# Moving part of a column sum from TensorE to VectorE in a prefix-sum kernel that streams 285 MB

## The chip, the cores and the metric

One core of a Trainium2 chip runs the kernel. The metric is device time in microseconds from start to end of one execution; the profile's span is some 1.7 us shorter, as it runs from the first to the last instruction. Ratios are computed as the mean time of one kernel's fast runs over the mean of the other's fast runs of the same rounds on the same chip, so they are not quite the ratios of the medians quoted beside them.

## The reference

```python
def reference(x):                      # x: (4, 4224, 4224) float32
    ps = np.cumsum(np.cumsum(x, axis=1), axis=2)
    diag = np.diagonal(ps, axis1=1, axis2=2)
    return np.cumsum(diag, axis=1).astype(np.float32)     # (4, 4224)
```

Every element of x with row and column up to i counts in the i-th diagonal value. All of x has to be read: 4 x 4224 x 4224 x 4 bytes = 285.5 MB.

## The kernel before

Columns are in 11 groups of 384. A batch is loaded as five strips of 768 rows, six rows to a partition, and a half strip of 384 rows, converted to bfloat16 on the way, into three strip buffers. The last batch is cut differently at its end, to shorten the work after the last byte.

```python
NBUF = 3
strips = ctx.enter_context(tc.tile_pool(name="strips", bufs=NBUF))
...
def load_rows(o, b, r0):                          # issued on GpSimd's queue
    f = o.shape[1]
    nc.gpsimd.dma_start(
        out=o, in_=x[b, r0 : r0 + f * P, :].rearrange("(p f) w -> p f w", f=f)
    )
...
def add_up(strip, f, r0, acc, um, wp=0, ws=None):
    nw = f * P // GW
    g = r0 // GW
    hi = r0 + f * P
    for j in range(g + nw, NG):                   # TensorE: column sums right of the block
        for q in range(f):
            columns(j, 0, GW, strip[:, q, j * GW : (j + 1) * GW], q > 0)
    ...
    mu = mup.tile([P, f, f * P], BF16, name=f"mu{f}")
    block = strip[:, :, r0:hi]                    # VectorE: the block on the diagonal
    nc.vector.tensor_mul(out=mu, in0=block, in1=um)
    nc.vector.tensor_sub(out=block, in0=block, in1=mu)
    for h in range(nw):
        for q in range(f):
            columns(g + h, 0, GW, mu[:, q, h * GW : (h + 1) * GW], q > 0)
    for q in range(f):                            # ScalarE: row sums of the left part
        if ws > wp:
            act_sum(acc[:, q, 0:1], strip[:, q, wp:ws])
    row_sums(acc[:, :, 1], strip[:, :, ws:hi])    # VectorE: row sums of the rest
...
# end of the last batch
weigh_b(dtot, weights, start=True)
weigh_a(ones_col[0:1], c12[0:1, 1, :], start=True)
weigh_b(ones_col[0:1], c12[0:1, 1, M0:])
...
nc.vector.tensor_copy(out=yl[:, :M0], in_=fin_a)
nc.sync.dma_start(out=out[b, T0 : T0 + M0].unsqueeze(0), in_=yl[:, :M0])
```

`columns` is a matmul with a one-hot selector, which adds the column sums of 384 columns to one row of `d` in PSUM. Six rows per partition take six of them. VectorE's `row_sums` is the last reader of most strips; when it is done, the buffer is free and GpSimd issues the load of the strip three places on.

Of the kernel before, what the change touches and what calls it, by code (L numbers as in the profile page):

```python
# [8 lines left out]
FP32 = mybir.dt.float32  # L9
# [8 lines left out]
def kernel(  # L18
# [14 lines left out]
    nc = tc.nc  # L33
# [3 lines left out]
    P = 128  # L37
    F = 3
    F2 = 2 * F
    GW = P * F  # L40
    NG = N // GW
# [7 lines left out]
    consts = ctx.enter_context(tc.tile_pool(name="consts", bufs=1))  # L49
    strips = ctx.enter_context(tc.tile_pool(name="strips", bufs=NBUF))  # L50
    mup = ctx.enter_context(tc.tile_pool(name="mup", bufs=1))
# [19 lines left out]
    def strip_tile():  # L71
        return strips.tile([P, F2, N], BF16, name="strip")

    def load_rows(o, b, r0):
# [4 lines that stand above are left out]
# [8 lines left out]
    sel = consts.tile([P, 2 * NG - 1], BF16, name="sel")  # L87
# [3 lines left out]
    def upper_mask(f):  # L91

        um = consts.tile([P, f, f * P], BF16, name=f"um{f}")
        nc.vector.memset(um, 1.0)  # L94
        nc.gpsimd.affine_select(  # L95
            out=um,
            in_=um,
            compare_op=ALU.is_gt,
            fill=0.0,
            base=0,  # L100
            pattern=[[-1, f], [1, f * P]],
            channel_multiplier=-f,
        )
        return um

    um6 = upper_mask(F2)
    um3 = upper_mask(F)
# [3 lines left out]
        out=um1,  # L111
        in_=um1,
# [10 lines left out]
        out=ident,  # L123
        in_=ident,
# [13 lines left out]
    def counted(name, rows, width, pieces):  # L138

        ti = consts.tile([P, GW], I32, name="counted")[:rows, :width]  # L140
        for c0, c1, base, step, cm in pieces:
            nc.gpsimd.iota(
                ti[:, c0:c1],
                pattern=[[step, c1 - c0]],
                base=base,
                channel_multiplier=cm,
            )
        tf = consts.tile([rows, width], FP32, name=name)
        nc.gpsimd.tensor_copy(out=tf, in_=ti)
        return tf  # L150
# [6 lines left out]
    def between_groups(name, turned):  # L157
# [25 lines left out]
    weights = counted("weights", P, GW, [(0, GW, 1, 1, -1)])  # L183
    nc.gpsimd.affine_select(
        out=weights,
        in_=weights,
# [12 lines left out]
        out=steps, in_=steps, scalar=2, op=ALU.arith_shift_right  # L199
# [7 lines left out]
    def matmul(o, lhsT, rhs, start=False):  # L207
        nc.tensor.matmul(  # L208
            o, lhsT=lhsT, rhs=rhs, start=start, stop=False, skip_group_check=True
        )  # L210

    def matmul_on(o, lhsT, rhs):

        te = nc.tensor
        te.add_instruction(  # L215
            mybir.InstMatmult(
                start_tensor_calc=False,
                stop_tensor_calc=False,
                tile_position=(0, 0),
                tile_size=(P, P if lhsT.shape[-1] > 64 else 32),  # L220
                bass_skip_group_check=True,
                ldweights=False,
                name=nc.get_next_instruction_name(),
                engine=te.engine,
                ins=[
                    te.lower_ap(rhs, opt=False),
                    te.lower_ap(lhsT, opt=False, for_matmul_weights=True),
                ],
                outs=[te.lower_ap(o)],
            )  # L230
        )
# [3 lines left out]
    ones_col = consts.tile([P, 1], FP32, name="ones_col")  # L235
# [11 lines left out]
    def act_sum(acc, src):  # L247
        w = src.shape[-1]
        dump = dumpool.tile([P, 2176], BF16, name="dump")
        nc.scalar.activation(  # L250
            out=dump[:, :w], in_=src, func=ACT.Copy, accum_out=acc
        )

    def row_sums(acc, src):
        nc.vector.reduce_sum(out=acc, in_=src, axis=AX.X)  # L255
# [18 lines left out]
    def masked(o, i, m, acc):  # L274
        nc.vector.scalar_tensor_tensor(  # L275
            out=o,
            in0=i,
            scalar=1.0,
            in1=m,
            op0=ALU.mult,  # L280
            op1=ALU.mult,
            accum_out=acc,
        )

    def scalar_cols(r0):

        return r0 * 9 // 16 // 32 * 32
# [22 lines left out]
    for b in range(B):  # L310
        whole = b < LB
        t0 = 0 if whole else 1
        r6, r3 = rows6[b % 2], rows3[b % 2]
        d = psum_d.tile([NG, GW], FP32, name="d")
# [6 lines left out]
        def row_of(j):  # L321
            return (j + t0) % NG

        def columns(j, lo, hi, rhs, same=False):


            k = row_of(j)
            lhsT = sel[:, NG - 1 - k : 2 * NG - 1 - k]
            if same:
                matmul_on(d[:, lo:hi], lhsT, rhs)  # L330
                return
            matmul(d[:, lo:hi], lhsT, rhs, start=first[0])
            first[0] = False

        def add_up(strip, f, r0, acc, um, wp=0, ws=None):


            nw = f * P // GW
            g = r0 // GW
            hi = r0 + f * P  # L340
            for j in range(g + nw, NG):
                for q in range(f):
                    columns(j, 0, GW, strip[:, q, j * GW : (j + 1) * GW], q > 0)
            if ws is None:
                ws = scalar_cols(r0)
            mu = mup.tile([P, f, f * P], BF16, name=f"mu{f}")
            block = strip[:, :, r0:hi]
            nc.vector.tensor_mul(out=mu, in0=block, in1=um)  # L348
            nc.vector.tensor_sub(out=block, in0=block, in1=mu)  # L349
            for h in range(nw):  # L350
                for q in range(f):
                    columns(g + h, 0, GW, mu[:, q, h * GW : (h + 1) * GW], q > 0)
            for q in range(f):
                if ws > wp:
                    act_sum(acc[:, q, 0:1], strip[:, q, wp:ws])
            row_sums(acc[:, :, 1], strip[:, :, ws:hi])

        acc6 = smalls.tile([P, NS, F2, 2], FP32, name="acc6")
# [10 lines left out]
        for s in range(ns):  # L369
            strip = prefetched.pop(0) if prefetched else None  # L370
            if strip is None:
                strip = strip_tile()
                load_rows(strip, b, s * F2 * P)
            add_up(strip, F2, s * F2 * P, acc6[:, s], um6)
            if not whole and s == 0:
                diag_b = last.tile([P, P], BF16, name="diag_b")
                nc.gpsimd.dma_start(out=diag_b, in_=x[b, TB:N, TB:N])
            if not whole and s == 1:
                row_sums(hs[:, 2:3], diag_b)
                masked(hmu[:, 2, :P], diag_b, um1[:, :P], hu[:, 2:3])  # L380
                nc.vector.tensor_sub(out=dtot, in0=hs[:, 2:3], in1=hu[:, 2:3])
                for h in range(3):
                    columns(LG, h * P, GW, hmu[:, h, : GW - h * P], h > 0)
        a6 = acc6[:, :ns]
        sum_up(a6)
        for h in range(2):
            ps = slice(h * HP, (h + 1) * HP)
            k = row_of(h)
            nc.vector.tensor_copy(  # L389
                out=r6[ps, k : k + 2 * ns : 2, :], in_=a6[ps, :, :, 1]  # L390
            )

        strip = strip_tile()
# [5 lines left out]
        else:  # L399
# [8 lines left out]
            wp, ws = 1280, 1280 + 1536  # L408
# [6 lines left out]
        if not whole:  # L415

            strip = strip_tile()
# [7 lines left out]
            for sb, c0, c1 in (  # L425
# [6 lines left out]
                r0 = TB + sb * R  # L432
                nc.gpsimd.dma_start(
                    out=part_b[:, sb, c0:c1],
                    in_=x[b, r0 : r0 + R, :TB].rearrange("r (k c) -> r k c", k=4)[
                        :, :, c0:c1
                    ],
# [18 lines left out]
        c12 = smalls.tile([NG, 2, GW], FP32, name="c12")  # L456
# [9 lines left out]
        for i, src in enumerate((d, c12[:, 0, :])):  # L466
            nc.vector.tensor_tensor_scan(  # L467
                out=c12[:, i, :],
# [8 lines left out]
            out=out[b, : j1 * GW].rearrange("(g i) -> g i", i=GW),  # L477
            in_=c12[t0:NG, 1, :],
# [5 lines left out]
        M0 = 2 * P  # L484
        E0 = GW - R
        fin_a = psum_s.tile([1, M0], FP32, name="fin_a")
        fin_b = psum_s.tile([1, P], FP32, name="fin_b")
        fin_e = psum_s.tile([1, R], FP32, name="fin_e")
        yl = last.tile([1, GW], FP32, name="yl")
        ye = last.tile([1, R], FP32, name="ye")  # L490

        def weigh_a(rows, w, start=False):

            matmul(fin_a, rows, w[..., :M0], start=start)

        def weigh_b(rows, w, r0=0, start=False):

            matmul(fin_b[:, r0:], rows, w[..., : P - r0], start=start)
# [7 lines left out]
        by = last.tile([P, P], FP32, name="by")  # L506
        nc.scalar.copy(out=by, in_=by_ps)
        weigh_b(dtot, weights, start=True)
        weigh_a(ones_col[0:1], c12[0:1, 1, :], start=True)
        weigh_b(ones_col[0:1], c12[0:1, 1, M0:])  # L510


# [1 line left out]
        arows = last.tile([P, 2], FP32, name="arows")  # L514
        nc.vector.tensor_add(out=arows, in0=asum[:, :, 0], in1=asum[:, :, 1])
        weigh_b(ones_col, by)
        weigh_a(arows[:, 0:1], weights)
        matmul(fin_a[:, P:], arows[:, 1:2], weights[:, :P])
        weigh_b(arows[:, 0:1], weights[:, M0:])
        weigh_b(arows[:, 1:2], weights[:, P:])  # L520
# [5 lines left out]
        pair_sum(bsum[:, 0, 1:2], part_b[:, 1, 512:])  # L526
        for i in (1, 0):
            weigh_b(bsum[:, 0, i : i + 1], weights4, R)
        nc.vector.tensor_copy(out=yl[:, :M0], in_=fin_a)
        nc.sync.dma_start(  # L530
            out=out[b, T0 : T0 + M0].unsqueeze(0), in_=yl[:, :M0]
        )
# [2 lines left out]
        for i in (1, 0):  # L535
# [8 lines left out]
            out=out[b, T0 + M0 : T0 + E0].unsqueeze(0), in_=yl[:, M0:E0]  # L544
# [35 lines left out]
```

## Time and profile before

| | before |
|---|---|
| median of the first three runs | 667.75 us (667.42 to 669.84) |
| span of the profiled run | 666.1 us |
| busy: VectorE / TensorE / ScalarE / GpSimd | 333.8 / 209.2 / 136.1 / 31.3 us |
| read from HBM | 285.47 MB |

The DMA row is the only one that is full. The page's first part (busy time, share of the span, instructions of each engine) and its summary of the chain that ended last name VectorE most often:

```profile
PE 209.2 (31%) x998; PEld 99.5 (15%) x998; DVE 333.8 (50%) x163; ACT 136.1 (20%) x219; POOL 31.3 (5%) x59
...
DVE 44%; another core or an unknown queue 41%; DMA 13%; PE 2%; issue 1%; DVEq 0%; POOLq 0%
```

Half of VectorE's time is idle, and the 41% "unknown" are waits for strips.

### The profile page before, as it was taken

To read this page: it belongs to the slowest core of one execution; us is meant where nothing else is said; L and a number is where in the kernel's file an instruction comes from. 1 tells how busy PE (TensorE), PEld (TensorE's weight loads), DVE (VectorE), ACT (ScalarE), POOL (GpSimd) and SP (SyncE) were. 2 spreads that over 40 slices of the span, in tenths; PEclk is the share of its full clock that TensorE was granted. 3 is DMA by queue.
4 is the path that set the end of the run, shared out by engine and by line. 5 is a ranking of instruction groups with operands and counts; after the bars stand their busy time and mean duration, and the time that the engine had idled before them with its cause. 6 is when DMAs were issued, how large, how long until landed. Compare 5 with 4: busy or idle time off the path is not lost.

```text
span 666.1 us, 2585 instructions
## 1 busy us (share of the span) xinstructions
PE 209.2 (31%) x998; PEld 99.5 (15%) x998; DVE 333.8 (50%) x163; ACT 136.1 (20%) x219; POOL 31.3 (5%) x59
## 2 busy tenths in 40 slices
PE   0071522403118153140320724414022253250428
PEld 0030211201003021010110312201011021120203
DVE  3160625456916153454782524436388343352766
ACT  0001121406300103040630020304063002030434
POOL 7000000000000000000000000000000000001000
PEclk9995857566558585765655958567565595765759
DMA  9999999999999999999999999999999999999998
GB/s 203 219 219 219 213 216 213 213 218 219 219 220 218 219 216 213 219 213 216 218 219 217 219 218 216 217 216 219 213 218 218 218 219 217 216 217 216 218 207 163
DMA packets 7673, 143.25 MB, mean 215 GB/s; under 512 B 704, under 2 KB 1004, under 8 KB 2156
## 3 DMA queue, kind: packets, MB, share of 16 engines
q0 software_dynamic: 7296, 142.47, 99.9%
q1 hardware_dynamic: 364, 0.61, 0.3%
q8 instruction: 8, 0.13, 0.1%
q14 instruction: 5, 0.04, 0.0%
HBM read 285.47 MB, written 0.07 MB: 429 GB/s over the span
## 4 chain that ended last, share of the span: by engine, by line
DVE 44%; another core or an unknown queue 41%; DMA 13%; PE 2%; issue 1%; DVEq 0%; POOLq 0%
DVE acc L255 27%; DMA strip<-in_x_dram 13%; DVE mu L348 7%; DVE strip L349 7%; DVE c L467 1%; PE d L208 1%; PE fold_a L215 0%; DVE pu L255 0%; DVE c L275 0%; PE fold_a L208 0%; PE fin_b L208 0%; PE fin_a L208 0%; DVE acc L364 0%; DVE rows L389 0%
## 5 line engine op out<-in xcount | busy, mean ns | idle before, releaser
L250 ACT ACTIVATE dump<-strip 128x416 bf16<-128x416 bf16 (+6 forms) x108 | 124.4, 1151 | 520.8 <-DMA strip<-in_x_dram 518.1
L348 DVE TENSOR_TENSOR mu<-strip,um 128x4608 bf16<-128x4608 bf16 (+1 forms) x24 | 52.4, 2183 | 307.5 <-DMA strip<-in_x_dram 307.4
L255 DVE TENSOR_REDUCE acc<-strip 128x6 f32<-128x4608 bf16 (+6 forms) x23 | 196.0, 8523 | 0.8
L208 PE MATMUL d<-strip,sel 128*11 128x384 bf16 x102 | 42.3, 415 | 375.8 <-DMA strip<-in_x_dram 375.8
L215 PEld LDWEIGHTS <-sel 128*11 128x11 bf16 x703 | 72.2, 103 | 502.8 <-issue 469.8
L215 PE MATMUL d<-strip,sel 128*11 128x384 bf16 x501 | 131.9, 407 | 0.0
L349 DVE TENSOR_TENSOR strip<-strip,mu 128x4608 bf16<-128x4608 bf16 (+1 forms) x24 | 52.4, 2183 | 1.0
L215 PE MATMUL d<-mu,sel 128*11 128x384 bf16 x200 | 43.9, 352 | 0.0
L76 POOL DMA_DIRECT2D strip<-in_x_dram x24 | 16.5, 688 | 543.4 <-DVE acc L255 281.4
L208 PE MATMUL d<-mu,sel 128*11 128x384 bf16 x43 | 15.6, 363 | 45.7 <-DVE mu L348 45.7
L250 ACT ACTIVATION_READ_ACCUMULATOR dump<-strip 128x1 f32 x108 | 20.1, 186 | 0.0
L208 PEld LDWEIGHTS <-sel 128*11 128x11 bf16 x146 | 14.6, 100 | 18.9 <-issue 10.1
L208 PE MATMUL d<-ident,rows 128*11 128x128 f32 x24 | 5.2, 380 | 16.8 <-DVE rows L398 16.8
L94 DVE MEMSET um<- 128x4608 bf16 (+1 forms) x2 | 4.9, 2458 | 1.1 <-issue 1.1
L208 PEld LDWEIGHTS d<-ident,rows 128*11 128x11 f32 x24 | 2.6, 119 | 18.9 <-DVE rows L398 11.7
L95 POOL TENSOR_SCALAR_AFFINE_SELECT um<-um 128x4608 bf16<-128x4608 bf16 (+1 forms) x2 | 5.2, 2613 | 2.4 <-DVE um L94 2.4
L208 PE MATMUL d<-halves,rows 128*11 128x64 f32 x48 | 5.3, 288 | 0.0
L255 DVE TENSOR_REDUCE pu<-d 11x1 f32<-11x384 f32 x4 | 2.2, 546 | 5.7 <-PE d L208 5.7
L208 PEld LDWEIGHTS d<-halves,rows 128*11 128x11 f32 x48 | 4.8, 128 | 1.3 <-issue 1.1
L215 PEld LDWEIGHTS <-ident_h 128*128 128x128 bf16 x18 | 2.1, 114 | 13.7 <-issue 12.7
L467 DVE TENSOR_TENSOR_SCAN c<-ones_row,carry,c 11x384 f32<-11x384 f32 x4 | 4.0, 1005 | 0.1
L467 DVE TENSOR_TENSOR_SCAN c<-ones_row,carry,d 11x384 f32<-11x384 f32 x4 | 4.0, 1001 | 0.1
(100 smaller groups left out, 51.3 us busy)
## 6 DMA issues: line engine op xcount, KB each, us to landing
strip<-in_x_dram POOLq DMA_DIRECT2D x19, 6336.0 KB, 76.5
strip<-in_x_dram POOLq DMA_DIRECT2D x5, 3168.0 KB, 59.7
strip<-in_x_dram POOLq DMA_DIRECT2D x1, 1080.0 KB, 49.9
strip<-in_x_dram POOLq DMA_DIRECT2D x1, 768.0 KB, 52.9
strip<-in_x_dram POOLq DMA_DIRECT2D x3, 256.0 KB, 54.1
head<-in_x_dram SPq DMA_DIRECT2D x1, 528.0 KB, 3.7
strip<-in_x_dram POOLq DMA_DIRECT2D x1, 192.0 KB, 43.2
strip<-in_x_dram POOLq DMA_DIRECT2D x1, 64.0 KB, 28.6
```

The source lines that it names most:

```text
L76: nc.gpsimd.dma_start(out=o, in_=x[b, r0 : r0 + f * P, :].rearrange("(p f) w -> p f w", f=f))
L94: nc.vector.memset(um, 1.0)
L95: nc.gpsimd.affine_select(out=um, in_=um, compare_op=ALU.is_gt, fill=0.0, base=0, pattern=[[-1, f], [1, f * P]], channel_multiplier=-f,)
L208: nc.tensor.matmul(o, lhsT=lhsT, rhs=rhs, start=start, stop=False, skip_group_check=True)
L215: te.add_instruction(mybir.InstMatmult(start_tensor_calc=False, stop_tensor_calc=False, tile_position=(0, 0), tile_size=(P, P if lhsT.shap ...
L250: nc.scalar.activation(out=dump[:, :w], in_=src, func=ACT.Copy, accum_out=acc)
L255: nc.vector.reduce_sum(out=acc, in_=src, axis=AX.X)
L348: nc.vector.tensor_mul(out=mu, in0=block, in1=um)
L349: nc.vector.tensor_sub(out=block, in0=block, in1=mu)
L467: nc.vector.tensor_tensor_scan(out=c12[:, i, :], data0=ones_row, data1=src, initial=carry[:, i : i + 1], op0=ALU.mult, op1=ALU.add,)
```

## The change

The intent is to take work from TensorE. In strips two to five of the three whole batches (12 strips), the first column group to the right of the diagonal block is summed over its six rows by VectorE, and one float32 matmul replaces six bfloat16 ones. At the end, a small matmul that added the scanned row is replaced by an addition in the copy that VectorE makes anyway.

```diff
+    sel_f = consts.tile([P, 2 * NG - 1], FP32, name="sel_f")
+    nc.vector.tensor_copy(out=sel_f, in_=sel)
...
-            for j in range(g + nw, NG):
+            for j in range(g + nw + by_rows, NG):
...
+            if by_rows:
+                rowed = mup.tile([P, GW], FP32, name="rowed")
+                row_sums(
+                    rowed,
+                    strip[:, :, hi : hi + GW].rearrange("p q c -> p c q"),
+                )
             for h in range(nw):
                 for q in range(f):
                     columns(g + h, 0, GW, mu[:, q, h * GW : (h + 1) * GW], q > 0)
+            if by_rows:
+                k = row_of(g + nw)
+                matmul(d, sel_f[:, NG - 1 - k : 2 * NG - 1 - k], rowed)
...
-            add_up(strip, F2, s * F2 * P, acc6[:, s], um6)
+            add_up(
+                strip, F2, s * F2 * P, acc6[:, s], um6, by_rows=whole and s > 0
+            )
...
-        weigh_a(ones_col[0:1], c12[0:1, 1, :], start=True)
...
-        weigh_a(arows[:, 0:1], weights)
+        weigh_a(arows[:, 0:1], weights, start=True)
...
-        nc.vector.tensor_copy(out=yl[:, :M0], in_=fin_a)
+        nc.vector.tensor_add(out=yl[:, :M0], in0=fin_a, in1=c12[0:1, 1, :M0])
```

More of the change, by code (lines that the diff above doesn't have):

```diff
@@ L333, in columns, with add_up @@
             first[0] = False
-        def add_up(strip, f, r0, acc, um, wp=0, ws=None):
+        def add_up(strip, f, r0, acc, um, wp=0, ws=None, by_rows=False):
             nw = f * P // GW
```

## The prediction

> **What bounds the kernel now.** I began with the page's slices, because the shares of busy time (VectorE 50%, TensorE 31%) name no engine that is full.
>
> ```profile
> DVE  3160625456916153454782524436388343352766
> DMA  9999999999999999999999999999999999999998
> GB/s 203 219 219 219 213 216 213 213 218 219 219 220 218 219 216 213 219 213 216 218 219 217 219 218 216 217 216 219 213 218 218 218 219 217 216 217 216 218 207 163
> ```
>
> The DMA engines are at nine tenths or more in all but the last slice, and the rate hardly moves. VectorE swings from 0 to 9 tenths under it without a mark: the eleventh slice, with VectorE at 9, has 219 GB/s, the fourth, with VectorE at 0, has 219 too. Those GB/s count bfloat16 bytes as written; what is read is float32, twice as much. x is 4 x 4224 x 4224 x 4 bytes = 285.5 MB, which the page confirms as 285.47 MB of HBM reads. Over the 666.1 us span that is 429 GB/s.
>
> Next the table of stretches, cut where strips arrive (start:end, length, busy time and count of PE, PEld, DVE, ACT, POOL, then clock, DMA share, GB/s):
>
> ```profile
> 35.00:65.00 30.00, 12.56 (x67) 6.27 (x66) 10.01 (x4) 0.13 (x1) 0.78 (x1) 0.78 1.01 216
> 125.30:155.10 29.80, 7.56 (x30) 3.39 (x30) 16.47 (x3) 8.17 (x12) 0.70 (x1) 0.61 1.01 218
> 662.00:663.00 1.00, 0.89 (x10) 0.55 (x9) 0.88 (x4) 0.73 (x3) 0.00 (x0) 1.00 0.47 71
> 663.00:664.00 1.00, 0.83 (x10) 0.38 (x10) 0.56 (x5) 0.64 (x3) 0.00 (x0) 1.00 0.00 1
> ```
>
> A six-row strip arrives every 29.8 to 30.4 us, while VectorE works 10.0 us in one interval and 16.5 us in another. The data stream ends near 662.5 us. So the span is about 1.3 us until the first load is issued, 661 us of streaming, and 3.6 us after the last byte.
>
> The chain of waits seems to say something else, "DVE 44%", and has to be read with care. Around the end of a batch it runs:
>
> ```profile
> 187.56 1.00 DVE c L467
> 188.58 11.89 another core or an unknown queue
> 200.49 2.57 DVE mu L348
> ```
>
> The 11.89 us piece is VectorE sitting idle until the next strip has landed; the view of waits puts 307.4 us of idle VectorE before the masked product down to the strip's DMA. The chain goes through VectorE's work merely because its successor on that engine stands next to it.
>
> The remaining question is whether VectorE, which gives strip buffers back, sets when loads are issued. GpSimd's timeline has the issues:
>
> ```profile
> 142.50 0.70 POOL L76 DMA_DIRECT2D strip<-in_x_dram  x1 [31.48 <-DVE acc L255]
> 174.47 0.72 POOL L76 DMA_DIRECT2D strip<-in_x_dram  x1 [31.27 <-ACT dump L250]
> 183.35 0.72 POOL L76 DMA_DIRECT2D strip<-in_x_dram  x1 [8.16 <-issue]
> ```
>
> The load issued at 142.50 is the first strip of the second batch, which lands at 200.49; the half strip before it is in at 170.2. So it was in the queue 27.7 us before the queue could run dry. The one issued at 174.47 had until 200.49, 26.0 us; the one at 183.35 until the strip at 230.4, 47 us. The smallest reserve in a batch is about 26 us. VectorE's release decides the issue, but not the arrival.
>
> **What the Trainium skill says.** "DMA: Bandwidth & Descriptors", section "Bandwidth", gives a fabric ceiling of 435 GB/s and measures 425 GB/s for a large load on a single core; it also gives 358 GB/s per core as an HBM limit. The trace sides with the first: from 34.88 to 200.49 us, 5.5 strips of 12.98 MB (6336 KB of bfloat16, twice that read) make 431 GB/s. It differs in that the bytes written to SBUF are only half of that. There is about 1% left to gain in the stream, and this change does not touch it.
> "VectorE: DVE Perf Modes", section "The perf-mode tier table", has tensor_reduce at one element per cycle whatever the type and tensor_tensor on bfloat16 at two. The trace agrees: row sums of 4608 and 10752 elements take 4953 and 11353 ns, a slope of 1.042 ns per element and about 153 ns fixed; the product of 4608 takes 2558 ns, 0.52 ns per element net of a similar start.
> "SBUF — State Buffer", section "Door 1: The DMA port swizzle", says that consecutive accesses should stay in a 16-byte line, or pay an unstated penalty. No large VectorE instruction of the kernel before steps so far; the new sum does: its six terms lie 8448 bytes apart.
> The same page, "Who interferes with whom", has DMA and compute engines on separate SBUF ports and says that tensor_reduce on this chip does not hold up GpSimd's descriptors. The slices above agree as to the rate, and the issues take 0.55 to 0.83 us with or without VectorE busy.
>
> **The change, part by part.** By program order on each engine, nothing else is moved.
> 1. VectorE gains 12 sums of 6 rows x 384 columns = 2304 elements (strips 2 to 5 of the three whole batches), placed between the subtraction and the row sums. At one element per cycle: 2304 x 1.042 + 153 = 2553 ns, 30.6 us in all. If each far step costs a second cycle: 2304 x 2.083 + 153 = 4953 ns, 59.4 us in all. Nothing in the trace chooses; I lean to the second, about 55 to 45. VectorE's busy time then goes from 333.8 to 364 or 393 us.
> 2. TensorE loses 72 bfloat16 matmuls of 384 columns and gains 12 float32 ones. In the timeline six of the old kind follow one another at 0.163 us where the clock is full and 0.32 us where it is throttled, so 0.98 to 1.92 us a strip. The float32 matmuls of 128 columns on the final d appear as two records each, six records in 0.76 us, so 0.99 ns per column and record; for 384 columns in two records 0.76 us, or about 1.5 us throttled. TensorE saves 0.2 to 0.4 us a strip, 3 to 5 us in all, on an engine that waits 375.8 us for strips.
> 3. The release of each such strip moves by 2.6 or 5.0 us, since VectorE is the last reader there. It does not add up from strip to strip, because VectorE is idle again each time: 13 to 18 us before the next six-row strip, and 11.9 us after the half strip, which follows the fifth strip without a gap. The reserve of 26 us becomes 21 to 23. Path cost: 0.
> 4. The batch's end (scan and output) moves later by the same 2.6 to 5.0 us, out of the 11.9 us gap. In the last batch no strip is summed by rows. Path cost: 0.
> 5. The float32 copy of the selector at the start runs while VectorE waits for the first strip until 34.88. Path cost: 0.
> 6. At the end, one matmul of 1 x 256 leaves the TensorE queue, 0.52 us in the chain of waits, and the copy to yl becomes an addition of the same 256 columns (0.41 us before). This is in the last 6 us, so I looked at it there:
>
> ```profile
> 660.32 0.59 PE L208 MATMUL fin_a<-c,ones_col 1*1 1x256 f32 x2
> 662.12 0.41 DVE L529 COPY yl<-fin_a 1x256 f32<-1x256 f32 x1 [1.04 <-PE fin_a L208]
> 662.46 0.44 DVE L264 SCALAR_TENSOR_TENSOR pair<-strip 128x288 f32<-128x288 bf16 x1
> 662.88 0.39 DVE L264 SCALAR_TENSOR_TENSOR pair<-strip 128x224 f32<-128x224 bf16 x1
> 662.94 0.47 ACT L250 ACTIVATE dump<-strip 128x320 bf16<-128x320 bf16 x1 [0.26 <-DMA strip<-in_x_dram]
> ```
>
> The addition may start about 0.5 us sooner, and the 288-wide pair about 0.4 us. But the 224-wide pair needs the same piece of the last rows for which ScalarE is waiting until 662.94. It can't start much before 662.88. So at most 0.1 us is left of it at the end.
>
> Sum: 0 + 0 + 0 - 0.1 = -0.1 us, from 667.75 to 667.6 us.
>
> **The rivals.**
> - VectorE's longer hold on strips makes loads start late. For it: most loads in GpSimd's timeline wait on "DVE acc". Against it: the reserve of 26 us is five to ten times the delay. Only a sum of over some 12 us (more than 5 cycles per element), which would first fill the 11.9 us gap at the end of a batch and then eat into the reserve, could come near. At 26 us a strip the batch of 165.6 us, with VectorE busy for about 84 us of it, would be VectorE-bound; that would cost over 20 us a batch and give over 720 us. I hold it under 1%.
> - The extra reads of SBUF slow the DMA's writes. A 1% lower rate is 6.6 us: 674 us. The constant rate under a VectorE at 0 and at 9 tenths speaks against it; the far-stepped pattern is new, which leaves about 2%.
> - The shorter tail counts in full: 0.4 to 0.5 us less, 667.3 us. For it, the chain of waits does pass through fin_a and yl; against it, the landing at 662.94. About 15%. It makes no difference to the verdict.
> - Less TensorE work raises the granted clock (0.662 on average) and so the speed. But TensorE waits for strips; only the last 8 us could use it, and there the clock is already 0.83 to 1.00, and these strips are not in the last batch. Worth 0.
>
> **Range and chances.** The three runs before lie between 667.42 and 669.84, so the scatter is larger than every term of the sum. I take 667.6, with 666.8 to 669.2 for eight in ten: half a microsecond of better tail below, one run of scatter above. Two per cent is 13.4 us, which only the first two rivals reach or half reach: faster 0.005, same 0.98, slower 0.015.
>
> **What would show it right or wrong.** Right: strips still land every 30 us at 216 to 218 GB/s and the DMA row stays at 9; a new group of 12 reductions 128x384 at about 2.6 or 5.0 us; the idle time of VectorE before its masked product falls from 307 by about the time of these sums; GpSimd's issues follow 2.6 to 5 us later without a gap in the stream; the 224-wide pair starts less than 0.5 us after the last piece has landed and the span is within 2 us of 666.1. Wrong: a slice with DMA under 9 before the last two, a strip interval over 31 us in the first three batches, or a sum of rows over 10 us.

## The result, and the profile after

The changed kernel took 668.03 us (median of six runs, 667.26 to 668.70), the kernel before 668.94 us in its six (667.42 to 669.84). The ratio is 0.9989 with a 95% interval of 0.9972 to 1.0005: the same.

The slices of the changed kernel, to be held against those of before:

```profile
DVE  3161828476946173756794526466589433352766
DMA  9999999999999999999999999999999999999998
GB/s 203 219 219 219 219 219 218 218 209 210 219 220 219 218 220 219 218 216 215 209 219 219 219 216 219 219 218 216 213 213 219 219 216 216 219 218 218 215 206 162
```

VectorE is busier in the first three quarters, and the DMA row has not changed. The stretches (start:end, length, then busy time and count of PE, PEld, DVE, ACT, POOL, clock, DMA share, GB/s) say it in numbers:

```profile
35.00:65.00 30.00, 13.29 (x68) 6.53 (x67) 10.10 (x4) 0.51 (x2) 0.77 (x1) 0.80 1.01 216
125.30:155.10 29.80, 6.39 (x26) 2.53 (x25) 20.29 (x4) 8.11 (x12) 0.70 (x1) 0.61 1.01 218
```

In the fourth strip's interval VectorE works 20.29 us instead of 16.47, and the strip still comes in the same 29.8 us at 218 GB/s. The whole difference is the new group of instructions (line, engine, operation, names, shapes, count; busy us, mean ns; idle before):

```profile
L258 DVE TENSOR_REDUCE rowed<-strip 128x384 f32<-128x2304 bf16 x12 | 49.0, 4082 | 0.0
```

Twelve sums take 49.0 us. VectorE's busy time rises by 47.0 us, from 333.8 to 380.8 (in the timeline each sum overlaps its two neighbours by nearly 0.2 us together, which is the difference), and the view of waits has its idle time before the masked product at 260.3 us instead of 307.4: 47.1 us less. The added busy time went into idle time one for one. The chain at the end of the first batch shows where (start, us, what):

```profile
192.35 7.61 another core or an unknown queue
199.99 2.57 DVE mu L351
```

The idle piece has shrunk from 11.89 to 7.61 us, and the next strip is there at 199.99, as it was at 200.49. GpSimd's timeline, with the three issues that answer to those of before:

```profile
146.25 0.70 POOL L76 DMA_DIRECT2D strip<-in_x_dram  x1 [31.45 <-DVE acc L258]
178.15 0.71 POOL L76 DMA_DIRECT2D strip<-in_x_dram  x1 [31.19 <-DVE acc L376]
187.12 0.71 POOL L76 DMA_DIRECT2D strip<-in_x_dram  x1 [8.26 <-issue]
```

Each load is issued 3.7 to 3.8 us later (142.50, 174.47 and 183.35 before), and arrives when it did. The tightest one, at 178.15, is 21.8 us ahead of the strip in front of it. Last, the end of the changed kernel:

```profile
661.57 0.41 DVE L542 TENSOR_TENSOR yl<-fin_a,c 1x256 f32<-1x256 f32 x1 [0.56 <-PE fin_a L211]
...
662.35 0.39 DVE L267 SCALAR_TENSOR_TENSOR pair<-strip 128x224 f32<-128x224 bf16 x1
...
662.41 0.47 ACT L253 ACTIVATE dump<-strip 128x320 bf16<-128x320 bf16 x1 [0.28 <-DMA strip<-in_x_dram]
...
663.61 0.23 SPq L562 DMA_DIRECT2D out_dram<-ye  x1
```

The last output is issued at 663.61 instead of 664.14. But the piece of rows that ScalarE was waiting for also came 0.53 us sooner, 662.41 instead of 662.94. From that landing to the last issue it is 1.20 us in both. The stream ended sooner in this execution, and the end itself is no shorter.

### The profile page after: what moved, and what is told of

Same layout as the page of the kernel before. It is cut to its first block, busy times and chain, and to the rows that moved or that the text cites. A ratio compares the mean times of both kernels' runs of the same rounds, so it can differ in the third digit from the quotient of the medians.

```text
span 665.6 us, 2495 instructions
## 1 busy us (share of the span) xinstructions
PE 206.6 (31%) x948; PEld 94.1 (14%) x948; DVE 380.8 (57%) x176; ACT 136.1 (20%) x219; POOL 31.3 (5%) x59
## 4 chain that ended last, share of the span: by engine, by line
DVE 54%; another core or an unknown queue 37%; DMA 5%; PE 3%; issue 1%; DVEq 0%; POOLq 0%
DVE acc L258 28%; DVE mu L351 8%; DVE strip L352 8%; DVE rowed L258 7%; DMA strip<-in_x_dram 5%; DVE c L481 1%; PE d L211 1%; PE fold L218 0%; PE d L218 0%; DVE pu L258 0%; DVE c L278 0%; DVE rows L403 0%; DVE acc L376 0%; PE fold_a L218 0%
## 5 line engine op out<-in xcount | busy, mean ns | idle before, releaser
L351 DVE TENSOR_TENSOR mu<-strip,um 128x4608 bf16<-128x4608 bf16 (+1 forms) x24 | 52.4, 2184 | 260.4 <-DMA strip<-in_x_dram 260.3
L218 PEld LDWEIGHTS <-sel 128*11 128x11 bf16 x643 | 66.7, 104 | 482.5 <-issue 453.6
L211 PE MATMUL d<-strip,sel 128*11 128x384 bf16 x90 | 37.3, 415 | 295.8 <-DMA strip<-in_x_dram 295.8
L218 PE MATMUL d<-strip,sel 128*11 128x384 bf16 x441 | 116.6, 408 | 0.0
L211 PE MATMUL d<-mu,sel 128*11 128x384 bf16 x43 | 16.3, 379 | 108.5 <-DVE mu L351 108.5
L258 DVE TENSOR_REDUCE rowed<-strip 128x384 f32<-128x2304 bf16 x12 | 49.0, 4082 | 0.0
L218 PE MATMUL d<-mu,sel 128*11 128x384 bf16 x200 | 46.7, 369 | 0.0
L211 PE MATMUL d<-rowed,sel_f 128*11 128x384 f32 x24 | 11.5, 566 | 20.3 <-DVE rowed L258 20.3
L211 PEld LDWEIGHTS <-sel 128*11 128x11 bf16 x134 | 13.6, 102 | 19.3 <-issue 12.3
L211 PEld LDWEIGHTS d<-rowed,sel_f 128*11 128x11 f32 x24 | 1.5, 91 | 24.9 <-DVE rowed L258 24.6
```

What stands on the lines that cost most here:

```text
L211: nc.tensor.matmul(o, lhsT=lhsT, rhs=rhs, start=start, stop=False, skip_group_check=True)
L218: te.add_instruction(mybir.InstMatmult(start_tensor_calc=False, stop_tensor_calc=False, tile_position=(0, 0), tile_size=(P, P if lhsT.shap ...
L258: nc.vector.reduce_sum(out=acc, in_=src, axis=AX.X)
```

## The experiments

The theory: the stream of x sets the time, and the third strip buffer is a reserve of some 22 us that hides how long VectorE holds a strip. Eleven kernels test it and the rivals; all but one, wrong on purpose, gave the right result.

### No work at all on 12 strips

```diff
-            add_up(strip, F2, s * F2 * P, acc6[:, s], um6)
+            if whole and s > 0:
+                nc.vector.memset(acc6[:, s], 0.0)
+            else:
+                add_up(strip, F2, s * F2 * P, acc6[:, s], um6)
```

> The kernel before, wrong on purpose: strips two to five of the three whole batches are loaded but not worked on at all (no matmuls, no products, no row sums). My theory (the stream of x is the bound): within 1.5 us of the kernel before, with VectorE's busy time near halved; so no saving on TensorE or VectorE, this change's included, could have made the kernel faster by more than that. Rival (the waits of loads on VectorE cost something already): several us faster.

It took 667.76 us (667.14 to 669.67) beside 668.74 us of the kernel before; ratio 0.9994, interval 0.9969 to 1.0018. Its slices of VectorE and DMA:

```profile
DVE  3160000000606000000071500000007243352766
DMA  9999999999999999999999999999999999999998
```

VectorE is at 149.6 us of busy time, TensorE at 107.8, and nothing is gained. ScalarE, too, falls from 136.1 to 50.5 us. So nothing that a change takes off these three engines in these strips can be worth more than the scatter.

### The sums four times, and six times

```diff
-                row_sums(
-                    rowed,
-                    strip[:, :, hi : hi + GW].rearrange("p q c -> p c q"),
-                )
+                for _ in range(4):          # 6 in the second kernel
+                    row_sums(
+                        rowed,
+                        strip[:, :, hi : hi + GW].rearrange("p q c -> p c q"),
+                    )
```

> The changed kernel (three buffers) with each sum of six rows done four times into the same tile: 36 more sums, 147 us more of VectorE, busy about 528 us. My theory: the release of strips moves by 12.2 us more, still inside the reserve of some 22 us, and VectorE's work in a batch of 165.6 us is about 84 + 4 x 16.3 = 149 us: no cost, within 1.5 us of the changed kernel. A rival that has far-stepped reads slow the DMA's writes by 1% while they run would show 147 us x 1% = 1.5 us or more and a lower rate in the slices; a rival in which VectorE's time counts would show up to 147 us.

> The changed kernel with each sum of six rows done six times: VectorE's work in a whole batch is about 84 + 6 x 16.3 = 182 us, over the 165.6 us that the loads of the batch take, and the sums hold each strip 20 us longer. My theory: here the reserve is used up and VectorE becomes the bound of the three whole batches: a cost of 16 us at least per batch and, with the order of the loads counted, up to 27 us: 715 to 750 us. If four times costs nothing and six times costs that, the limit lies where the reserve says. Rival (the loads have still more reserve than I read): 668 to 690 us.

Four times: 667.96 us (667.52 to 668.33) beside 667.71 us; ratio 1.0004, interval 0.9989 to 1.0019. Its slices:

```profile
DVE  3160999999998299999999829999999973352766
DMA  9999999999999999999999999999999999999998
```

VectorE is busy 524.9 us, is at nine tenths for most of the whole batches, and the time is the same. The fifth strip's buffer is now given back for an issue at 194.28 us:

```profile
194.28 0.71 POOL L76 DMA_DIRECT2D strip<-in_x_dram  x1 [33.83 <-DVE acc L377]
```

That is some 7 us before the stream would run dry at about 201 us (the half strip in front has landed at 171.17 us, and a six-row strip takes 29.9), where 21.8 us were left with one sum. The issue moved by 16.1 us (from 178.15), not by the 12.2 expected: the fifth strip had landed by 156.16, but VectorE was still at the fourth and began it at 159.03. With sums this long the delays do add up from strip to strip. The rival in which far-stepped reads slow the DMA falls too: 48 sums, 193.9 us of them, and two strip intervals fully covered by VectorE have 217 and 219 GB/s.

Six times: 751.83 us (751.12 to 752.07) beside 668.74 us, ratio 1.1242. Its slices of the DMA:

```profile
DMA  9999999992939999999297799999957949999998
GB/s 202 216 218 220 218 222 215 219 204 54 218 74 207 217 219 220 216 219 216 46 195 151 149 218 216 216 216 216 216 112 146 201 87 217 218 216 216 216 217 158
```

The holes have come. Between 170 and 180 us not a byte arrives, while VectorE is busy for all ten. The cost is 83 us, or 28 us a batch; I had written 16 to 27, so the size was a little over the range. The limit lies between 16 and 24 us of sums per strip. This pair of runs alone doesn't say that the reserve sets it: with six sums VectorE's work in a batch, about 182 us, is also more than the 165.6 us that its loads take. What the reserve is worth is shown by the next runs, in which VectorE's work stays below that.

### Two buffers instead of three

```diff
-    NBUF = 3
+    NBUF = 2
```

This edit was made to the kernel before and to the changed kernel. In a third kernel, the changed one with two buffers, the fifth strip is also left out of the new sum:

```diff
-                strip, F2, s * F2 * P, acc6[:, s], um6, by_rows=whole and s > 0
+                strip, F2, s * F2 * P, acc6[:, s], um6, by_rows=whole and 0 < s < NS - 1
```

> The kernel before with two strip buffers in place of three. My theory (the third buffer is the reserve that hides VectorE): with two, the load of the next batch's first strip is issued only when VectorE gives back the fifth strip, 18.7 us after that landed (155.2 to 173.9 us before), while the half strip behind it takes only 14.9 us. The stream stands still for 18.7 - 14.9 = 3.8 us plus the start of a load[...], so 4 to 7 us at each of three batch ends: 12 to 20 us more than the kernel before, 680 to 689 us. If the loads were not tied to VectorE's release in this way, 668 us.

> The changed kernel with two strip buffers. My theory: without the reserve the sum of six rows in the fifth strip (4.08 us) stands in the stream in full, three times: 3 x 4.08 = 12.2 us more than the kernel before with two buffers, 692 to 701 us; the sums in the second to fourth strips cost nothing, since their release leaves 9 us and more before the queue is dry. Rival (the sums are hidden because TensorE's saving pays for them, or because they touch nothing that loads wait for): the same as the kernel before with two buffers, within 2 us.

> The changed kernel with two buffers, with the sum by rows in the second to fourth strips only (9 sums, the fifth strip as before). My theory: the same as the kernel before with two buffers within 1.5 us, since only the fifth strip's release is followed by a short load. Rival (every microsecond of VectorE counts alike once the reserve is gone): 9 x 4.08 = 37 us more than it; or, if the cost of the changed one is spread evenly, three quarters of that.

| two buffers | median | range |
|---|---|---|
| kernel before | 693.27 us | 692.61 to 694.45 |
| changed | 703.63 us | 703.15 to 704.54 |
| changed, without the fifth strip | 692.63 us | 692.43 to 693.89 |

All three ran beside 667.71 us with three buffers. The stretches around the end of the first batch, for the kernel before and then for the changed one:

```profile
170.00:175.00 5.00, 0.00 (x0) 0.00 (x0) 5.00 (x1) 3.59 (x3) 0.00 (x0) 0.50 0.00 0
175.00:180.00 5.00, 2.40 (x15) 1.58 (x14) 4.75 (x7) 2.66 (x4) 0.70 (x1) 0.50 0.71 127
```

```profile
170.00:175.00 5.00, 0.00 (x0) 0.00 (x0) 5.00 (x1) 4.71 (x5) 0.00 (x0) 0.50 0.00 0
175.00:180.00 5.00, 0.69 (x3) 0.32 (x3) 4.78 (x6) 1.54 (x2) 0.70 (x1) 0.50 0.42 61
```

The stream stands still while VectorE finishes the fifth strip, and stands still longer with the sum in it. With the reserve gone, the change costs 703.63 - 693.27 = 10.4 us, near the 3 x 4.08 = 12.2 us expected. Without the fifth strip, nine sums out of twelve cost nothing at all (692.63 beside 693.27 us). So it is not VectorE's time that counts there, but the release of one strip, the one behind which only a half strip is queued.

My number for the kernel before was too low: 25.6 us instead of 12 to 20, 8.5 us a batch instead of 4 to 7. I had counted from the landing of the half strip. Its landing is when ScalarE starts on it, 171.38 us, but from 168 to 170 us only 25 GB/s still moved, and from 170 us on nothing. The bulk of its data was there some 3 us before the landing counted, and with nothing queued behind it those 3 us are lost too. The next load is issued at 175.68 and moves its first bytes after 177 us, so the stream all but stands still from 168 to 177 us, 9 us, which is near the 8.5. The reserve of 21.8 us is therefore some 5 us smaller in use than it looks (3 us of landing and 1 to 2 us from issue to first bytes), and with four sums perhaps 2 us of the 7 were left. Both are estimates.

### What one far step costs

Five more sums, of the same 2304 elements to 384 totals, in the first strip of each whole batch; their results are overwritten:

```diff
+            if whole and s == 0:
+                probe = mup.tile([P, GW], FP32, name="rowed")
+                flat = strip[:, 0, : F2 * GW]
+                nc.vector.reduce_sum(out=probe, in_=flat.rearrange("p (c q) -> p c q", q=F2), axis=AX.X)
+                nc.vector.reduce_sum(out=probe.rearrange("p (a r) -> p a r", r=4), in_=flat.rearrange("p (a q r) -> p a r q", q=F2, r=4), axis=AX.X)
+                nc.vector.reduce_sum(out=probe.rearrange("p (a r) -> p a r", r=16), in_=flat.rearrange("p (a q r) -> p a r q", q=F2, r=16), axis=AX.X)
+                nc.vector.reduce_sum(out=probe, in_=flat.rearrange("p (q c) -> p c q", q=F2), axis=AX.X)
+                nc.vector.reduce_sum(out=probe, in_=strip[:, :, N - GW : N].rearrange("p q c -> p c q"), axis=AX.X)
```

> The changed kernel with five more sums of 2304 elements to 384 totals in the first strip of each whole batch, which differ only in how far apart the six terms of a total lie: 2, 8, 32, 768 and 8448 bytes. Theory A (a cost for each access to another 16-byte line): 2.55 us at 2 bytes, between that and 4.1 us at 8 bytes, 4.1 us from 32 bytes on. Theory B (the cost lies in 384 totals of only six terms): 4.1 us for all five. Theory C (distance matters): 32 and 768 bytes cheaper than 8448. The time is that of the changed kernel, as 15 to 20 us more in the first strip stays in its reserve of over 40 us.

The timeline of VectorE in the first strip, the steps being 2, 8, 32, 768 and 8448 bytes in this order (start, duration in us):

```profile
46.59 2.54 DVE L392 TENSOR_REDUCE rowed<-strip 128x384 f32<-128x2304 bf16 x1
49.16 2.55 DVE L393 TENSOR_REDUCE rowed<-strip 128x384 f32<-128x2304 bf16 x1
51.75 4.25 DVE L394 TENSOR_REDUCE rowed<-strip 128x384 f32<-128x2304 bf16 x1
56.03 4.02 DVE L395 TENSOR_REDUCE rowed<-strip 128x384 f32<-128x2304 bf16 x1
60.08 4.02 DVE L396 TENSOR_REDUCE rowed<-strip 128x384 f32<-128x2304 bf16 x1
```

Of the three theories A fits best: from 32 bytes on some 1.5 to 1.7 us are paid, at 8448 bytes no more than at 32 or 768. At 8 bytes nothing is paid, where A had something between. Theory B falls with the first two lines, theory C with the last three. Why 32 bytes cost 0.23 us more than 768 was not asked. The cost of a step is (4.02 - 2.54) us / 2304 = 0.64 ns, less than the second cycle (1.04 ns) of the prediction. The boundary lies between 8 and 32 bytes; a step of 16 bytes was not tried, so that it is a 16-byte line is not shown here. The single run took 668.31 us: VectorE was busy for 432.5 us, 51.7 us more than in the changed kernel, and once more no difference is to be seen.

### The end of the change alone

```diff
-        weigh_a(ones_col[0:1], c12[0:1, 1, :], start=True)
...
-        weigh_a(arows[:, 0:1], weights)
+        weigh_a(arows[:, 0:1], weights, start=True)
...
-        nc.vector.tensor_copy(out=yl[:, :M0], in_=fin_a)
+        nc.vector.tensor_add(out=yl[:, :M0], in0=fin_a, in1=c12[0:1, 1, :M0])
```

> The kernel before with only the end of the change (one matmul less, addition in place of the copy). My theory: nothing, because the 224-wide pair still waits for the last pieces: from ScalarE's start on the 320-wide piece to the issue of the last output 1.20 us as in both traces, and a time within the scatter of the kernel before. Rival (the shorter chain counts): 0.7 to 0.8 us from that start to that issue, or an end 0.4 to 0.5 us earlier for the same end of the stream; the addition to yl starts some 0.5 us earlier in both views.

It took 667.53 us (667.26 to 667.65) beside 668.74 us: ratio 0.9982, interval 0.9968 to 0.9997. That interval leaves out 1, which my theory doesn't allow for, while the trace has 1.21 us from the landing to the last issue, as before. So it was run again, with an unchanged copy of the kernel before and the changed kernel beside it (no edit but a comment line):

> The kernel before against itself, to learn the scatter on this chip. Both theories: a ratio of 1 within 0.2%; single runs between 667.2 and 669.9 us. If some runs of either copy come out near 669.5 and others near 667.5, as in the kernel before so far, that is scatter of one and the same program.

> The end of the change alone, once more, because its four runs were all at 667.3 to 667.7 us beside 667.5 to 669.6 us of the kernel before (ratio 0.9982). My theory: ratio 1 within 0.2%, and again 1.20 us from ScalarE's start on the 320-wide piece to the issue of the last output. Rival (the new end avoids the runs near 669.5 us): no run above 668.8 us out of six, while the kernel before and its copy have some; ratio 0.998 to 0.999.

> The changed kernel once more beside these. My theory: ratio 1 within 0.2%, the same as both copies of the kernel before. Rival: as for the end alone, no run above 668.8 us and a ratio of 0.998 to 0.999.

| against the kernel before on the same chip (668.34 us, 667.52 to 669.62) | median | range | ratio | 95% interval |
|---|---|---|---|---|
| the kernel before, a copy | 667.79 us | 667.37 to 668.20 | 0.9986 | 0.9972 to 0.9999 |
| the end alone | 667.69 us | 667.46 to 668.24 | 0.9986 | 0.9972 to 0.9999 |
| the changed kernel | 668.37 us | 667.40 to 669.75 | 0.9996 | 0.9977 to 1.0015 |

The copy of the kernel before is "faster" than itself by just as much as the end alone. And the changed kernel has a run of 669.75 us, so the new end doesn't avoid those either. A difference of 0.14% is scatter of one program here, even where the interval says otherwise.

The copy's trace held something else:

```profile
662.64 0.41 DVE L530 COPY yl<-fin_a 1x256 f32<-1x256 f32 x1 [1.55 <-PE fin_a L209]
662.91 0.47 ACT L251 ACTIVATE dump<-strip 128x320 bf16<-128x320 bf16 x1 [0.28 <-DMA strip<-in_x_dram]
...
663.36 0.38 DVE L265 SCALAR_TENSOR_TENSOR pair<-strip 128x224 f32<-128x224 bf16 x1
...
664.54 0.23 SPq L550 DMA_DIRECT2D out_dram<-ye  x1
```

Here the 224-wide pair starts 0.45 us after its piece has landed, and the last output is issued 1.63 us after it instead of 1.20. The reason is an earlier piece: TensorE's products of it start 2.93 us before that landing instead of 3.47, so the chain through fin_a and yl came too late. In the changed kernel with two buffers the same piece was as late (2.94 us), and its end still took 1.21 us. In all nine traces with the new end it is 1.20 to 1.23 us; of the four with the old end three have 1.20 or 1.21 and this one 1.63. So the shorter end seems worth up to 0.4 us in some executions and nothing in others. That is 0.06% and was not to be seen in any time.

## Why the prediction was right

It said 667.6 us, in a range of 666.8 to 669.2, and "same" at 98%; it was 668.03 us and the same. That the number came within 0.4 us is luck, as runs of one kernel differ by up to 2.4 us; what was right is that every term costs nothing on the path, and why.

- **Step 1, the sums.** The sum was the one size left open between 2.55 and 4.95 us, with a lean to the larger. It measured 4.08 us, so VectorE rose to 380.8 us, between the 364 and 393 offered, and neither of the two sizes given as a sign of being right (2.6 or 5.0 us) came true. The idea of a cost per far step held, and the assumption of one whole further cycle was too much.
- **Step 2, TensorE.** Its busy time fell from 209.2 to 206.6 us, 2.6 us, and not 3 to 5. The low end was rounded up: 12 strips at 0.2 to 0.4 us are 2.4 to 4.8 us. That no one waits for it holds: with half of its work left out the time was the same.
- **Steps 3 and 4, the release and the end of a batch.** Issues moved by 3.7 to 3.8 us, the reserve went from 26.0 to 21.8 us, the gap from 11.89 to 7.61 us, and no strip came later. (The strips' spacing was read a little short: 64.9 to 95.4 us before the change is 30.5 us, not 30.4 at most.) That the delay does not add up from strip to strip holds for one sum, and no longer for four. The reserve was taken as the whole time from issue to the last landing, which the two-buffer runs put some 5 us too high. That it is the third buffer that pays for this is shown by the two-buffer runs, where the same sums cost 10.4 us.
- **Step 5, the float32 selector.** Nothing in the trace speaks against it: the first masked product starts with the first strip. It was not tested alone.
- **Step 6, the end.** Right in the traces that I compared, where 0.00 us was left of the 0.5. Said too firmly as a rule: one trace of the unchanged kernel has 0.43 us there, because the pieces of the last rows don't always land at the same distance.
- **The rivals.** VectorE's hold does become the bound, but later than I wrote: I had a sum over some 12 us coming near, and 16 us (four sums) still cost nothing, since both the gap and the reserve can be used up; 24 us cost 83 us. The slower stream did not appear at 48 sums. The gain from a higher granted clock didn't either: the clock was 0.654 instead of 0.662.

No version that beats both kernels came out of this. Taking the work out altogether gained nothing.

## What to carry to other kernels

Before moving work between engines, ask whether any engine's time reaches the end at all; here the row of slices answers it, since the only full one was the DMA. A chain that names an engine for half of the span may only be passing through it, and its idle pieces are room for more work; here even 16 us a strip were free beside pieces of some 11 to 18 us, as the buffers let work slip past the gap. The slack that buffers give is worked out as the time between a load's issue and the moment at which the queue would run dry, less what a load needs to start and to land (some 5 us here). While some of it is left a delay costs nothing; with two buffers, the three sums behind which the queue was dry, 12.2 us, cost 10.4 us, and the nine others nothing.

## What the Trainium skill lacked or had wrong

- "SBUF — State Buffer", section "Door 1: The DMA port swizzle", gives no size for leaving a 16-byte line. On VectorE's sums far steps cost 0.64 ns per element: 2.54 and 2.55 us at steps of 2 and 8 bytes, 4.02 us at 768 and 8448, 4.25 us at 32. Its remark that two hits per line are enough agrees with the 8-byte case; no run shows where between 8 and 32 bytes the cost begins.
- "VectorE: DVE Perf Modes", section "The perf-mode tier table", has tensor_reduce at one element per cycle with no word on what steps cost. That holds for near ones (1.04 ns per element); far ones took (4082 - 153) / 2304 = 1.71 ns.
- "DMA: Bandwidth & Descriptors", section "Bandwidth", places the ceiling of 435 GB/s at the ports into SBUF. With a load that converts to bfloat16, only some 216 GB/s are written there, and the number fits what is read, 431 GB/s. The sentence that for loads from HBM the limit of about 358 GB/s binds did not hold for this one core; the same section measures 425 GB/s on a single core and gives 358 as the share when both cores of a pair stream.
